# One row of sixteen places for weight units in a trunk layer with a mixture of experts: raw and split units share them, x1's place joins, the second biases run on four row groups, and the experts come in another order

## The chip, the cores and the metric

The kernel runs on one core of a Trainium2 chip. The metric is the device time of one execution in microseconds. Below, PE is the matrix engine, PEld its weight loads, DVE the vector engine, ACT the scalar engine, POOL the GpSimd engine, and SP the queue that issues the weight transfers. SBUF is the memory on the core from which the engines read; PSUM holds the results of products.

## The reference, cut to what matters

The layer takes 512 tokens of 1024 channels. A front part (input projection, a convolution branch, an mLSTM branch, output projection, layer norm) gives x1. Then 4 of 32 experts work on each token, and a second layer norm ends the layer:

```
logits = x1 @ router_w + router_b;  top 4 of 32;  gate = softmax(top 4)
for each expert e, for its tokens:
    h = x1[tok] @ w1[e] + b1[e]              # 1024 -> 2048, halves g and lin
    act = min(g, 7) * sigmoid(1.702 * min(g, 7)) * (clip(lin, -7, 7) + 1)
    acc[tok] += gate * (act @ w2[e] + b2[e])   # 1024 -> 1024
x = layer_norm(alpha * x1 + acc)
```

Everything is float32. An expert has 8 MB of w1 and 4 MB of w2, and all 32 are read: 384 MB.

## The kernel before

**Units.** Weights come in units of 1 MB (128 partitions x 2048 numbers): eight units of w1 (two halves of four: g, then lin) and four of w2 per expert, 384 in all. `Units.fetch` (line 249) issues one transfer on SP's queue into the next of eight raw places: raw2, raw, raw, raw3 three times, hl3 twice. A transfer can start when the last reader of what lay in its place is done, and SP issues in order: one transfer that waits holds all behind it.

**Blocks.** The experts are ranked by how many tokens they have, and a rank has fixed blocks of rows (`RANKS`): rank 0 has two blocks of 128, written (128, 128) below; ranks 1 to 3 have (128, 64); 4 to 7 one of 128; 8 to 12 (64, 32); 13 to 24 one of 64; 25 to 30 one of 32; the first expert in the order has one of 128. In the string `TURNS` these kinds are h (ranks 0 to 3), m, n, l and s. A block of 64 or 32 rows is multiplied in float32 straight from the raw unit (`product`, line 388), two or four column groups of the array side by side. A block of 128 rows needs the unit split into a high and a low half (`split`: ACT casts at line 273, DVE subtracts at line 276), and twelve products of three passes follow (line 400). A split unit takes two places of 8 KB per partition, from six more: hl2 twice and hl four times. A raw unit whose every block is small is held until its products are done; one that is split, until the subtraction is done.

I call an expert with a 128-row block large, and the others small. Each expert's turn on PE is one segment: four units of its w1, two units of the w2 of the expert before it, four units of w1, two units of that w2. A gate (`swiglu`) and turns of rows into columns (`turn`) lie between. `send` adds an expert's result to `ysum` in memory by a scatter on POOL. After the last expert `ysum` is loaded again (line 517) and the layer norm follows.

**Start.** The first eight units are fetched ahead, while the front part ends. The router (`Router.tile`) and the ranking (`Router.order`) run on DVE, ACT and PE. The first expert's first product needs their result.

**Second biases.** `bias2` adds gate-weighted rows of b2 to the sums in `xt`, which holds x1 times alpha (the trace calls this tile hT), and writes `xt` to `ysum`. It brings b2 into rank order by two products (line 1304); then for each of four groups of 128 tokens it turns the 32 gates into a column by one product (line 1310), takes two products with 32 rows of contraction (line 1315) and adds them (line 1317). It stands after the first expert's segment. After it `xt` is free until line 517, and holds 16 KB per partition: two places.

A scheduler of the framework, not the source alone, orders the instructions of each engine.

Of the kernel before, what the change touches and what calls it, by code (L numbers as in the profile page):

```python
# [5 lines left out]
F32 = mybir.dt.float32  # L6
F32R = mybir.dt.float32r
# [8 lines left out]
P = 128; T = 512; D = 1024; NT = 4; KD = 8; E = 32; TOPK = 4; F = 1024  # L16
# [7 lines left out]
def f32(ap):  # L24
    return ap.bitcast(F32)
# [216 lines left out]
class Units:  # L242
# [7 lines left out]
    def fetch(self, src):  # L250
        w = self.raws[self.f % len(self.raws)].tile([P, 2048], F32, name="raw")
        self.f += 1
        self.nc.sync.dma_start(w, src)
        return w
# [22 lines left out]
        return s  # L277

RANKS = [(P, P)] + [(P, 64)] * 3 + [(P,)] * 4 + [(64, 32)] * 5 + [(64,)] * 12 + [(32,)] * 6 + [(P,)]
# [7 lines left out]
    return [(sum(rows[:b]), rows[b]) for b in range(len(rows))]  # L290


TURNS = "lhslmnlhslmlnhslslnmlhslnmlnlsl"


def turns():

    kinds = dict(h=[1, 2, 0, 3], m=list(range(4, 8)), n=list(range(8, 13)), l=list(range(13, 25)), s=list(range(25, 31)))
    return [FIRST] + [kinds[k].pop(0) for k in TURNS]


# [4 lines left out]
def moe(tc, units, ahead, wr, wq, pp, ph, c, R, x1d, ysum, acc, w1, w2, B1, xg, early, bias2, last, xs, ne=E):  # L306
# [3 lines left out]
    nc = tc.nc  # L310
# [160 lines left out]
    for i, r in enumerate(seq):  # L471
        ev = 0 if r == FIRST else nc.sync.value_load(R.perm[0:1, r:r + 1], min_val=0, max_val=ne - 1)
        more = i + 1 < E
        if i == 0:
            gt, oh = gather(seq[1], 0, False)
            x1 = rows(oh)
            gts = [gather(r, 0, False)[0]]
            for t in range(NT):
                nc.scalar.activation(acc[:, t, :], acc[:, t, :], AF.Copy, scale=ALPHA)
        elif more:  # L480
            gt, g = gather(seq[i + 1], 0)
        acts = [width(m) for m in RANKS[r]]
        if acts[0] == F:
            acts = [wq.tile([P, F], F32, name="act", bufs=2)[:, 0:d] for d in acts]
        else:
            act = wq.tile([P, F], F32, name="act", bufs=2)
            acts = [act[:, i * 512:i * 512 + d] for i, d in enumerate(acts)]
        hold = {}
        for h, act, to in zip(gemm1(r, ev, 0, xs, hold), acts, gts):
            swiglu(h, act, 0, to)  # L490
        if pend is not None:
            pe, pa, pg = pend

            hs = [turn(a, *((wr, "xs") if b and a.shape[1] == F else (wq, "hs"))) for b, a in enumerate(pa)]
            ys = places(hs)
            gemm2(pe, 0, hs, ys)
        for h, act, to in zip(gemm1(r, ev, 1, xs, hold), acts, gts):
            swiglu(h, act, 1, to)
        if more:
            gtn, xs = [gt], [turn(g, wr, "xs") if i else x1]  # L500
            for b in range(1, len(blocks(seq[i + 1]))):
                gt, g = gather(seq[i + 1], b)
                gtn.append(gt)
                xs.append(turn(g, wr, "xs"))
        if pend is not None:
            gemm2(pe, 1, hs, ys)
            send(ys, pg)
        if i == 0:
            bias2()
        if i == 1:  # L510
            early()
        pend = (ev, acts, gts)
        if more:
            gts = gtn
# [11 lines left out]
    y = wq.tile([P, F], F32, name="sg", bufs=1)[:, 0:512]  # L526
# [3 lines left out]
    sums = [sums[t // 2][:, t % 2, :] for t in range(NT)]  # L530
# [655 lines left out]
    return B1  # L1186


class Other:


    def __init__(self, pool):
        self.pool = pool

    def tile(self, *_, **__):
        return f32(self.pool.tile([P, 2, 1024], F32R, name="hl")).rearrange("p a b -> p (a b)")


def body(tc, I, out, ne=E):
    nc = tc.nc  # L1200
    top = ExitStack()
# [94 lines left out]

    def bias2():

        b2 = wl.tile([P, D], F32, name="act", bufs=2)[0:E]
        nc.sync.dma_start(b2, I["b2"])  # L1300
        for n in range(2):
            cols = slice(n * 512, (n + 1) * 512)
            ps = pm.tile([P, 512], F32, name="tp", bufs=2)[0:E]
            nc.tensor.matmul(ps, R.sel[0:E, :], b2[:, cols], start=True, stop=True)
            nc.scalar.copy(b2[:, cols], ps)
        for t in range(NT):
            w = wl.tile([P, T], F32, name="gm", bufs=1)
            nc.vector.tensor_add(w[:, 0:E], f32(R.vals[:, t, :, 1]), f32(R.vals[:, t, :, 2]))
            tp = pm.tile([P, 4, P], F32, name="tp", bufs=2)
            nc.tensor.transpose(tp[0:E, 0, :], w[:, 0:E], c["ident"])  # L1310
            wT = w[0:E, P:2 * P]
            nc.scalar.copy(wT, tp[0:E, 0, :])
            for n in range(2):
                ps = pm.tile([P, 512], F32, name="tp", bufs=2)
                nc.tensor.matmul(ps, wT, b2[:, n * 512:(n + 1) * 512], start=True, stop=True)
                x = xt[:, t, n * 512:(n + 1) * 512]
                nc.vector.tensor_add(x, ps, x)
            nc.scalar.dma_start(ysum[t * P:(t + 1) * P], xt[:, t, :])

    fin = {}  # L1320

# [73 lines left out]
```

## Time and profile before

| | before |
|---|---|
| median of 3 runs | 1804.31 us (1802.85 to 1807.08) |
| the profiled execution's own time | 1804.05 us |
| its span, first to last instruction | 1802.2 us |
| mean granted clock of PE | 0.955 of full speed |
| PE, DVE, ACT, POOL busy | 92%, 53%, 31%, 13% |
| moved by DMA | 488.90 MB, mean 271 GB/s |

The busy share of PE is not its distance from a limit: a product that waits for nothing and one in a row of late transfers both count as busy. The line of DMA shares by slice tells more: low for the first 15 slices (the front part), then near 9 with some slices below it. The last weight product ends at 1758 us; what follows is the load of the sums, the layer norm and the stores.

### The profile page before, as it was taken

Reading aid. Unit: us, or ns where it says so; the run is one execution under the profiler, and the core shown is the slowest. Engines: PE = TensorE matmul, PEld = TensorE weight load, DVE = VectorE, ACT = ScalarE, POOL = GpSimd, SP = SyncE. Lnnn points to the kernel's source line nnn. Section 1 sums busy time; section 2 is a strip of 40 time slices with the busy share of each in tenths; the row PEclk is TensorE's granted clock in tenths of the full one; section 3 lists DMA queues with packets and bytes.
Section 4 is the critical chain, followed back from the end, with each engine's and each line's share of the span. In section 5 each row is a group of like instructions: output and inputs, shape, how many; then the busy total and the mean of one; then the engine's idle time right before and its main releaser. Section 6 shows DMA issues by size and latency. Waiting matters only on the chain. (4 is left out here: it accounts for less than half of the span.)

```text
span 1802.2 us, 22812 instructions
## 1 busy us (share of the span) xinstructions
PE 1660.1 (92%) x8840; PEld 1008.7 (56%) x8840; DVE 956.0 (53%) x1431; ACT 557.5 (31%) x739; POOL 237.4 (13%) x174
## 2 busy tenths in 40 slices
PE   7999999899999989989999899997899998999873
PEld 5878878688877836545454443762245543443321
DVE  5999998967567737335253543441135631442104
ACT  4442353334342515223232422320034421321001
POOL 0110031014112001010010200011111111001001
PEclk9999999899999869999999999999899999999986
DMA  5222221122255656999989999589999899999992
GB/s 192 94 71 91 85 94 71 47 94 94 95 182 191 276 192 226 371 402 414 396 303 395 400 415 398 215 334 393 411 414 409 298 357 400 402 360 378 401 400 91
DMA packets 77427, 488.90 MB, mean 271 GB/s; under 512 B 9808, under 2 KB 11616, under 8 KB 22434
## 3 DMA queue, kind: packets, MB, share of 16 engines
q1 hardware_dynamic: 65186, 458.80, 64.0%
q0 software_dynamic: 9104, 19.66, 4.8%
q10 hardware_dynamic: 3024, 8.94, 1.3%
q8 instruction: 71, 1.16, 0.3%
q14 instruction: 42, 0.34, 0.1%
HBM read 471.18 MB, written 19.33 MB: 272 GB/s over the span
## 5 line engine op out<-in xcount | busy, mean ns | idle before, releaser
L276 DVE TENSOR_TENSOR hl<-raw,hl 128x1024 fp32r<-128x1024 f32 x261 | 324.3, 1269 | 133.9 <-ACT hl L273 132.5
L273 ACT CAST hl<-raw 128x1024 fp32r<-128x1024 f32 x261 | 265.0, 1047 | 218.5 <-PE mm L742 78.2
L388 PE MATMUL h<-raw,xs 128*32 128x256 f32 (+1 forms) x2016 | 299.0, 499 | 20.9 <-DMA raw<-w 20.8
L742 PE MATMUL mm<-xhl,hl 128*128 128x512 f32 x1176 | 291.8, 403 | 8.9 <-ACT hl L273 8.9
L400 PE MATMUL h<-hl,xs 128*128 128x512 f32 x1008 | 255.4, 407 | 14.5 <-ACT hl L273 10.2
L742 PEld LDWEIGHTS mm<-xhl,hl 128*128 128x128 f32 x1176 | 224.7, 192 | 64.7 <-ACT hl L273 9.6
L400 PEld LDWEIGHTS h<-hl,xs 128*128 128x128 f32 x1008 | 190.6, 193 | 80.1 <-ACT hl L273 16.3
L388 PEld LDWEIGHTS h<-raw,xs 128*32 128x32 f32 (+1 forms) x2016 | 94.5, 125 | 189.9 <-issue 134.9
L799 DVE SCALAR_TENSOR_TENSOR acc<-zp,vec,acc 128x512 f32<-128x512 f32 x240 | 181.0, 768 | 2.0
L438 DVE TENSOR_SCALAR gm<-h 128x512 f32<-128x512 f32 (+2 forms) x41 | 30.7, 749 | 225.6 <-PE h L388 162.0
L388 PE MATMUL y<-raw,hs 128*32 128x256 f32 (+1 forms) x848 | 128.5, 500 | 9.3 <-DMA raw<-w 8.7
L342 POOL DMA_INDIRECT xg<-x1d,idx x39 | 60.6, 1553 | 550.3 <-DVE oh L325 292.1
L434 DVE TENSOR_SCALAR gm<-h 128x512 f32<-128x512 f32 (+2 forms) x41 | 30.7, 748 | 192.0 <-PE h L388 157.1
L460 POOL DMA_INDIRECT ysum<-yo,idx x40 | 65.8, 1646 | 474.7 <-ACT yo L459 366.1
L400 PE MATMUL y<-hl,hs 128*128 128x512 f32 x432 | 118.2, 419 | 6.7 <-DVE hl L276 3.6
L388 PE MATMUL h<-hl,xs 128*32 128x256 f32 (+1 forms) x672 | 102.3, 498 | 3.8 <-DMA hl<-w 3.8
L400 PEld LDWEIGHTS y<-hl,hs 128*128 128x128 f32 x432 | 80.8, 196 | 39.0 <-issue 10.1
L639 PE MATMUL mm<-hl,xhl 128*128 128x512 f32 x384 | 96.1, 403 | 1.7 <-ACT sg L792 1.5
L388 PEld LDWEIGHTS y<-raw,hs 128*32 128x32 f32 (+1 forms) x848 | 39.1, 124 | 80.6 <-issue 62.4
L639 PEld LDWEIGHTS mm<-hl,xhl 128*128 128x128 f32 x384 | 72.7, 191 | 19.0 <-ACT sg L792 1.8
L459 ACT COPY yo<-y 128x512 f32<-128x512 f32 (+2 forms) x36 | 22.1, 628 | 192.7 <-PE y L388 143.0
L435 ACT ACTIVATE sg<-gm 128x512 f32<-128x512 f32 (+2 forms) x41 | 27.8, 678 | 132.8 <-DVE gm L434 132.6
(309 smaller groups left out, 1594.0 us busy)
## 6 DMA issues: line engine op xcount, KB each, us to landing
raw<-w SPq DMA_DIRECT2D x288, 1024.0 KB
hl<-w SPq DMA_DIRECT2D x96, 1024.0 KB
raw<-wf SPq DMA_DIRECT2D x44, 1024.0 KB
cvp<-xT SPq DMA_DIRECT2D x8, 256.0 KB
hT<-x SPq DMA_DIRECT2D x1, 2048.0 KB
x1d<-hT ACTq DMA_DIRECT2D x4, 512.0 KB
ysum<-hT ACTq DMA_DIRECT2D x4, 512.0 KB
hT<-ysum SPq DMA_DIRECT2D x1, 2048.0 KB
```

Of the source, the lines that this page charges most:

```text
L273: nc.scalar.copy(s[:, 0, :], w)
L276: eng.tensor_sub(s[:, 1, :], w, f32(s[:, 0, :]))
L342: nc.gpsimd.indirect_dma_start(out=g, out_offset=None, in_=split_rows(x1d, m), in_offset=bass.IndirectOffsetOnAxis(ap=ix[:, 0:1], axis=0), ...
L388: nc.tensor.matmul(o[j * m:(j + 1) * m], x[:, 2 * u + k, :], w[:, k * 1024 + j * d:k * 1024 + (j + 1) * d], start=first and k == 0, stop=e ...
L400: nc.tensor.matmul(o[:, j, :], x[:, a, 2 * u + k, :], s[k][:, b, j * 512:(j + 1) * 512], start=first and k == 0 and i == 0, stop=end and k ...
L434: nc.vector.tensor_scalar(gm, h, LIMIT, None, op0=OP.min)
L435: nc.scalar.activation(sg, gm, AF.Sigmoid, scale=SW_ALPHA)
L438: nc.vector.tensor_scalar(gm, h, LIMIT, -LIMIT, op0=OP.min, op1=OP.max)
L460: nc.gpsimd.indirect_dma_start(out=split_rows(ysum, P * d // D), out_offset=bass.IndirectOffsetOnAxis(ap=ix[:, 0:1], axis=0), in_=o, in_of ...
L639: nc.tensor.matmul(ps, src[:, a, kk, t * P:(t + 1) * P], w[k][:, b, :], start=(kk == 0 and (a, b) == PASS[0]), stop=(kk == KD - 1 and (a, ...
L742: nc.tensor.matmul(ps, w[k][:, a, j * P:(j + 1) * P], mov[:, b, k, :], start=(k == 0 and (a, b) == PASS[0]), stop=(k == KD - 1 and (a, b) ...
L799: nc.vector.scalar_tensor_tensor(o, z[:, j:j + T], V("dw_w", m * CT + j), o, op0=OP.mult, op1=OP.add)
```

## The change

`Ring` takes the place of `Units` for the experts: one row of 14 places, from which raw units and split halves take the next in turn (`take`). A raw unit takes one place and a split one two more. When `bias2` is done it adds two places in `xt` at the front of the row (`more`); they take raw units only, since splits pass over them. So there are sixteen.

`bias2` now stands after the first half of the first expert's w1 in the source. The two products that rank b2 write it four times over, on four groups of 32 partitions; the gates of all four groups of tokens are turned by one product; and the products of the four groups of tokens read four row groups of the array and write four banks of PSUM. The write of `xt` to `ysum` follows after all sums.

The order of experts is another one. Before it was, after the first: l h s l m n l h s l m l n h s l s l n m l h s l n m l n l s l, with the (128, 128) expert as the third h. Now it is l m l l s h s n s h l l s h s l n n l l h l l m s n m m n l, with the (128, 128) expert as the first h.

```
+class Ring(Units):
...
+    def take(self, plain=False):
+
+        i = 0
+        while not plain and not isinstance(self.slots[i], tuple):
+            i += 1
+        p = self.slots[i]
+        del self.slots[i]
+        self.slots.append(p)
...
-TURNS = "lhslmnlhslmlnhslslnmlhslnmlnlsl"
+TURNS = "lmllshsnshllshslnnllhllmsnmmlnl"
...
-    kinds = dict(h=[1, 2, 0, 3], m=list(range(4, 8)), n=list(range(8, 13)), l=list(range(13, 25)), s=list(range(25, 31)))
+    kinds = dict(h=[0, 1, 2, 3], m=list(range(4, 8)), n=list(range(8, 13)), l=list(range(13, 25)), s=list(range(25, 31)))
...
+        if i == 0:
+            bias2()
         if pend is not None:
...
-        if i == 0:
-            bias2()
...
-    units = Units(nc, [raw2, raw, raw, raw3, raw3, raw3, Other(hl3), Other(hl3)], [hl2] * 2 + [hl] * 4, set())
+    units = Ring(nc, [(raw2, "raw")] + [(raw, "raw")] * 2 + [(raw3, "raw")] * 3 + [(hl3, "hl")] * 2 + [(hl2, "hl")] * 2
+                 + [(hl, "hl")] * 4)
...
+        b2, p2 = (wl.tile([P, D], F32, name="yo", bufs=2) for _ in range(2))
+        nc.sync.dma_start(b2[0:E], I["b2"])
...
+            nc.tensor.matmul(ps, sel, b2[0:E, cols], start=True, stop=True)
+            nc.scalar.copy(p2[:, cols], ps)
...
+            sums = [y[:, 0, :], y[:, 1, :]] + [pm.tile([P, 512], F32, name="tp", bufs=2) for _ in range(2)]
+            for t in range(NT):
+                part = slice(t * E, (t + 1) * E)
+                nc.tensor.matmul(sums[t], wT[part], p2[part, cols], start=True, stop=True)
+            for t in range(NT):
+                nc.vector.tensor_add(xt[:, t, cols], sums[t], xt[:, t, cols])
         for t in range(NT):
...
             nc.scalar.dma_start(ysum[t * P:(t + 1) * P], xt[:, t, :])
+        units.more([xt[:, 2 * k:2 * k + 2, :] for k in range(2)])
```

Three places show how instructions moved. The first is SP's queue of weight transfers, from the ninth unit on. Before, they stand like this (raw and hl are places, w1 and w2 the weights):

```order
L253 DMA raw_4598<-w1 128x2048
...
L253 DMA raw_4604<-w1 128x2048
...
L253 DMA raw_4610<-w1 128x2048
...
L253 DMA raw_4616<-w1 128x2048
...
L253 DMA raw_4643<-w2 128x2048
...
L253 DMA raw_4663<-w2 128x2048
```

Now, with hT_126 the tile `xt`:

```order
L1322 DMA yo_4437<-b2 32x1024
...
L301 DMA raw_4646<-w2 128x2048
...
L301 DMA hl_4710<-w2 128x2048
...
L301 DMA hT_126<-w1 128x2048
...
L301 DMA hT_126<-w1 128x2048
...
L301 DMA hl_4593<-w1 128x2048
```

Two units of w2 stand ahead; the second expert's first two units of w1 go into `xt`, which `bias2` must have written out by then, and all later units stand behind them.

The second place is PE's queue around `bias2`. Before (selc picks ranks, xs64 is the second expert's input, h_4595 its first result):

```order
L388 MATMUL h_4595<-raw_4616,xs64_4339 64x512 x4
...
L1304 MATMUL tp_4517<-act_4515,selc_3665 32x512
L1304 MATMUL tp_4520<-act_4515,selc_3665 32x512
L1310 MATMUL tp_4525<-ident_69,gm_4523 32x128
L1315 MATMUL tp_4528<-act_4515,gm_4523 128x512
L1315 MATMUL tp_4531<-act_4515,gm_4523 128x512
```

Now (h_4478 is the first expert's second half, h_4580 the second expert's first result):

```order
L431 MATMUL h_4478<-hl_4538,xs_4206 128x512 x6
L1329 MATMUL tp_4442<-yo_4437,gm_4440 128x512
L1329 MATMUL tp_4445<-yo_4437,gm_4440 128x512
L1335 MATMUL tp_4449<-ident_69,gm_4440 128x128
L1344 MATMUL y_4452<-yo_4438,gm_4440 128x512 x2
L1344 MATMUL tp_4453<-yo_4438,gm_4440 128x512
L1344 MATMUL tp_4454<-yo_4438,gm_4440 128x512
...
L419 MATMUL h_4580<-hT_126,xs64_4339 64x512 x8
```

The second expert's first half stood ahead of the biases and now stands behind them, since its weights come into `xt`.

The third place is DVE's queue while the router runs. Before (p0, first and x1T belong to the router):

```order
L155 CAST selb_3669<-sel_3899 128x96
L161 SCALAR_TENSOR_TENSOR p0_3905<-rt_3902,sel_3899 128x1
L162 TENSOR_SCALAR first_3671<-io1_74,p0_3905 128x128
L138 TENSOR_SCALAR x1T_4118<-tp_4120,ln1c_3676 128x128 x4
L143 TENSOR_TENSOR lg_4018<-rt_3991,rb_3659 128x32
```

Now:

```order
L155 CAST selb_3669<-sel_3899 128x96
L307 TENSOR_TENSOR raw_4414<-raw_4274,raw_4414 128x1024
L307 TENSOR_TENSOR raw_4417<-raw_4274,raw_4417 128x1024
L161 SCALAR_TENSOR_TENSOR p0_3905<-rt_3902,sel_3899 128x1
L307 TENSOR_TENSOR raw_4481<-raw_4276,raw_4481 128x1024
L162 TENSOR_SCALAR first_3671<-io1_74,p0_3905 128x128
L307 TENSOR_TENSOR raw_4484<-raw_4276,raw_4484 128x1024
L138 TENSOR_SCALAR x1T_4118<-tp_4120,ln1c_3676 128x128 x4
L143 TENSOR_TENSOR lg_4018<-rt_3991,rb_3659 128x32
L307 TENSOR_TENSOR raw_4499<-raw_4278,raw_4499 128x1024
```

Five subtractions of splits that stood behind the ranking now stand among the router's steps.

## Rows read from the trace of the kernel before

**Rows 1.** The page: busy share of DMA, in tenths, in 40 slices of the span

```profile
DMA  5222221122255656999989999589999899999992
```

**Rows 2.** Stretches: length, busy us (and instructions) by engine, PE clock, DMA share, GB/s

```profile
740.00:1758.00 1018.00, 939.35 (x5738) 464.09 (x5734) 367.95 (x518) 263.70 (x343) 121.00 (x75) 0.97 0.96 377
577.00:740.00 163.00, 151.77 (x706) 95.55 (x706) 96.20 (x183) 59.17 (x78) 10.64 (x16) 0.88 0.69 256
1180.00:1400.00 220.00, 195.66 (x1312) 95.43 (x1305) 62.32 (x105) 50.49 (x70) 27.91 (x19) 0.96 1.02 406
```

**Rows 3.** Stretches of 20 us with low DMA shares

```profile
920.00:940.00 20.00, 20.00 (x93) 12.07 (x93) 12.41 (x14) 8.03 (x9) 3.10 (x2) 1.00 0.62 216
...
1140.00:1160.00 20.00, 20.00 (x115) 13.12 (x114) 9.75 (x9) 7.06 (x9) 0.00 (x0) 1.00 0.31 122
...
1420.00:1440.00 20.00, 20.00 (x91) 12.13 (x88) 12.47 (x16) 8.63 (x10) 1.97 (x1) 1.00 0.68 250
```

**Rows 4.** Waits of SP's queue and of PE: us in total, times, longest

```profile
SPq L253 <- DVE hl L276: 603.2, 100, 31.8
...
PE h L388 <- DMA raw<-w: 20.8, 18, 1.9
PE h L400 <- ACT hl L273: 10.2, 6, 3.3
```

**Rows 5.** PE in order of time: start, length, line, product, records

```profile
693.21 11.32 PE L400 MATMUL h<-hl,xs 128*128 128x512 f32 x48
705.88 3.65 PE L388 MATMUL h<-raw,xs 128*64 128x512 f32 x16
741.30 3.63 PE L388 MATMUL h<-raw,xs 128*32 128x256 f32 x64
```

**Rows 6.** PE from the first expert's products to the end of the biases

```profile
603.06 10.37 PE L400 MATMUL h<-hl,xs 128*128 128x512 f32 x43
...
631.02 2.56 PE L400 MATMUL h<-hl,xs 128*128 128x512 f32 x10
...
637.82 4.50 PE L388 MATMUL h<-raw,xs 128*64 128x512 f32 x18
...
644.72 2.00 PE L1304 MATMUL tp<-act,selc 32*32 32x512 f32 x4 [1.85 <-DMA act<-b]
...
667.66 1.01 PE L330 MATMUL tp<-vals,oh 128*128 128x4 f32 x4
```

**Rows 7.** DVE: the router's steps, a subtraction of a split, an addition of biases

```profile
587.09 0.16 DVE L161 SCALAR_TENSOR_TENSOR p<-rt,sel 128x1 f32<-128x1 f32 x1 [0.39 <-PE rt L159]
590.97 1.37 DVE L138 TENSOR_SCALAR x1T<-tp,ln1c 128x128 f32<-128x128 f32 x4 [2.05 <-PE rt L141]
607.59 1.24 DVE L276 TENSOR_TENSOR hl<-raw,hl 128x1024 fp32r<-128x1024 f32 x1
649.64 0.69 DVE L1317 TENSOR_TENSOR hT<-tp,hT 128x512 f32<-128x512 f32 x1 [6.87 <-PE tp L1315]
```

**Rows 8.** SP's issues of weight units, x their number, around the biases

```profile
639.98 2.71 SPq L253 DMA_DIRECT2D raw<-w  x3
673.68 2.15 SPq L253 DMA_DIRECT2D hl<-w  x2
...
739.04 2.05 SPq L253 DMA_DIRECT2D hl<-w  x2
```

**Rows 9.** The end: last products, scatter, load of the sums, two row groups

```profile
1744.27 1.07 PE L388 MATMUL y<-raw,hs 128*32 128x256 f32 x16 [0.84 <-DMA raw<-w]
...
1746.24 1.58 POOL L460 DMA_INDIRECT ysum<-yo,idx  x1 [27.06 <-ACT yo L459]
...
1756.09 1.94 PE L388 MATMUL y<-hl,hs 128*64 128x512 f32 x8 [0.82 <-DMA hl<-w]
...
1770.35 0.69 PE L537 MATMUL h<-sg,gm 64*128 64x512 f32 x1
1770.36 0.69 PE L537 MATMUL tp<-sg,gm 64*128 64x512 f32 x1
```

More of the change, by code (lines that the diff above doesn't have):

```diff
@@ L277, in split, with __init__, more, fetch @@
         return s
+class Ring(Units):
+    def __init__(self, nc, slots):
+        self.nc, self.slots = nc, deque(slots)
+    def more(self, slots):
+        self.slots.extendleft(slots)
+    def take(self, plain=False):
[5 more added lines that the diff above has]
+        self.slots.append(p)
+        return f32(p[0].tile([P, 2, 1024], F32R, name=p[1])) if isinstance(p, tuple) else p
+    def fetch(self, src):
+        w = self.take(True).rearrange("p a b -> p (a b)")
+        self.nc.sync.dma_start(w, src)
+        return w
+    def split(self, w):
+        s = self.take().bitcast(F32R)
+        self.nc.scalar.copy(s[:, 0, :], w)
+        self.nc.vector.tensor_sub(s[:, 1, :], w, f32(s[:, 0, :]))
+        return s
 RANKS = [(P, P)] + [(P, 64)] * 3 + [(P,)] * 4 + [(64, 32)] * 5 + [(64,)] * 12 + [(32,)] * 6 + [(P,)]
@@ L1186, in bias_rows @@
     return B1
[L1189 to L1196, printed above, removed]
 def body(tc, I, out, ne=E):
@@ L1297, in bias2 @@
     def bias2():
-        b2 = wl.tile([P, D], F32, name="act", bufs=2)[0:E]
-        nc.sync.dma_start(b2, I["b2"])
+        b2, p2 = (wl.tile([P, D], F32, name="yo", bufs=2) for _ in range(2))
+        nc.sync.dma_start(b2[0:E], I["b2"])
+        w = wl.tile([P, F], F32, name="gm", bufs=1)
+        sel = w[0:E, 2 * P:3 * P]
+        nc.vector.tensor_copy(sel.rearrange("p (t e) -> p t e", t=NT), R.sel[0:E, None, :].to_broadcast([E, NT, E]))
         for n in range(2):
             cols = slice(n * 512, (n + 1) * 512)
-            ps = pm.tile([P, 512], F32, name="tp", bufs=2)[0:E]
-            nc.tensor.matmul(ps, R.sel[0:E, :], b2[:, cols], start=True, stop=True)
-            nc.scalar.copy(b2[:, cols], ps)
@@ L1306, in bias2 @@
-        for t in range(NT):
[L1307 to L1317, printed above, removed]
+            ps = pm.tile([P, 512], F32, name="tp", bufs=2)
@@ new lines, in bias2 @@
+            nc.tensor.matmul(ps, sel, b2[0:E, cols], start=True, stop=True)
+            nc.scalar.copy(p2[:, cols], ps)
+        nc.vector.tensor_add(w[:, 0:P].rearrange("p (t e) -> p t e", t=NT), f32(R.vals[:, :, :, 1]),
+                             f32(R.vals[:, :, :, 2]))
+        ps = pm.tile([P, 512], F32, name="tp", bufs=2)
+        nc.tensor.transpose(ps[:, 0:P], w[:, 0:P], c["ident"])
+        wT = w[:, P:2 * P]
+        nc.scalar.copy(wT, ps[:, 0:P])
+        for n in range(2):
+            cols = slice(n * 512, (n + 1) * 512)
+            y = pm.tile([P, 2, 512], F32, name="y", bufs=1)
+            sums = [y[:, 0, :], y[:, 1, :]] + [pm.tile([P, 512], F32, name="tp", bufs=2) for _ in range(2)]
[4 more added lines that the diff above has]
+                nc.vector.tensor_add(xt[:, t, cols], sums[t], xt[:, t, cols])
```

## The prediction, made before the changed kernel ran

> **What bounds the kernel now.** I read the DMA shares by slice first [rows 1], then the same by stretches, then the waits, then PE in order of time. From 740 us to the last weight product at 1758 the transfers run at a mean share of 0.96 and 377 GB/s, where a stretch in which they never stop shows 1.02 and 406 [rows 2]. So over 1018 us they stood still for about (1.02 - 0.96) / 1.02 x 1018 = 60 us. The stops lie together: three of the nine worst stretches of 20 us are in [rows 3], and the worst run, 1120 to 1180, is the segment of the (128, 128) expert. There PE is busy all the time and DMA at 0.31. SP waits mostly for subtractions that free a raw place [rows 4]. In the stretches between, PE waits for weights. So the limit changes hands: under a large expert PE is the bound and all eight raw places are full; under small ones the transfers are, and eight units of lead are soon used up. A larger lead is worth what the 60 us of stops are worth.
>
> Prices. A unit on a 128-row block takes PE 11.32 / 4 = 2.83 us, on 64 rows 3.65 / 2 = 1.82, on 32 rows 3.63 / 4 = 0.91 [rows 5] (a float32 product leaves two records: 16 are two units of a 64-row block, 64 are four of a 32-row block). A unit costs the transfers: 377 GB/s x 1018 us = 384 MB for the 347 units after 740, gathers and scatters among it, is 1.106 MB each, and at 406 GB/s 2.72 us. A segment of 12 units is 32.7 us of transfers. On PE, with some 3 us of turns, gathers and biases, a segment is 57 to 64 us for (128, 128), 47 to 51 for (128, 64), 34 to 38 for m and n, 21 to 28 for l, 17 to 20 for s behind a small one.
>
> **Term 1: the start.** Five subtractions of 1.24 us now stand among the router's steps. The first of them stands where p is at 587.09; DVE was idle 2.05 us for PE before x1T [rows 7], which swallows part of three or four. I take +3 us for the first expert's first product, so 606 for 603.06 (bounds 1 and 6). One of its splits now stands behind the gate of its first half on DVE: I take 4 us of wait on PE (0 to 6). Its products end at 633.6 before [rows 6], so near 641 now. Then the chain of the biases: 2.0 us for the ranking products [rows 6], two copies and a turn, some 1.7, four products side by side 1.0, eight additions of 0.69 [rows 7] with a second round of products among them, 6.5, and a subtraction of a w2 split that stands ahead of the additions, 1.5: sums complete near 653.5. Writing 2 MB at 406 GB/s is 5.2 us, with landing 6.5: the place is free near 660. Only then can SP issue the second expert's first unit, which lands after 2.72 + 2: PE goes on near 665. Before, it went on at 667.66 [rows 6], but had the second expert's first four units (8.5 us with the gather among them, up to 642.3) behind it. So PE stands 5 to 6 us later in its work.
>
> That the four products run side by side rests on the end of the trace: two products on two row groups into two banks start 0.01 us apart, and each takes 0.69 us [rows 9]. The Trainium skill (TensorEngine Tiling (Array Packing), "Gotcha 1: PSUM Pressure") says that row tiles can't use the same PSUM bank at once; here each group has a bank of its own, so by that rule too they run together. By it, if a bank were shared, the two rounds would cost eight products of 1.0 us for two, and the start 6 us more; the trace shows the first case for two groups, and nothing here shows four.
>
> For the transfers: before, 22 units were issued by 642.7, nothing till 673.7, and 38 by 734.4, which had landed by 740, with two more at 739 [rows 8]. Now 10 are issued by 645, nothing till 660, then one every 2.72 us, since no early segment stops them for long (l, m, l, l follow): 10 + (740 - 662) / 2.72 = 38.7 at 740. Equal: 0 us (bounds -8 and +15, three units and five).
>
> **Term 2: stops in the steady part.** From a given unit the row of places reaches sixteen units ahead if they are small, and 16 / 3 = five if they are large. At the end of a large expert come four small units, two of its w2 (three places each) and four small ones: 14 places, ten units. So while PE is in a (128, 128) segment of 57 us the lead can grow from three units to ten, and the transfers bring 12 + 7 = 19 units, 52 us: a stop of 5 for the 28.6 us of 1120 to 1180 before ([rows 3] for its middle). In a (128, 64) segment of 47 to 51 us they bring 17 or 18 units, 46 to 49 us: 0 to 3 us each, three times. The segments of m and n are 1 to 5 us above 32.7: what the lead doesn't take there, some 8 us over eight. One blocked transfer holds all behind it on SP, and a place that waits for a product of five units ago frees late at the entry of a large expert, where the old kernel had eight raw units and three split ones: some 10 us over nine large experts. Together 5 + 5 + 8 + 10 = 28, say 30 us for 60: -30 us (bounds -50 and 0).
>
> Splits reach five units ahead on PE where six places reached three, and so PE's waits for casts [rows 4] may fall by some us. No row shows such a row of places; I take 0.
>
> **Term 3: the end.** Before, the transfers were the bound to the last unit: PE waits 0.84 us before the s expert's last unit, whose product ends at 1745.3, 0.82 before the last of all [rows 9]; from 1745.3 to the end, through scatter and load, it is 56.9 us. That chain stays. Now m m n l n l stand at the end: PE takes 37.5 + 37.9 us for 65.4 of transfers in the two m segments, and 62 in the last two. So it ends with a lead of some three units: the last expert but one is done 3 x 2.72 = 8 us later against the last transfer than before. It sends two blocks for one, and a scatter holds POOL 1.58 us [rows 9]. +10 us (bounds 0 and +14).
>
> **Sum.** 1802.2 + 0 - 30 + 10 = 1782.2 us of span; the execution's time is 1.85 above its span, 1784; the median of the runs is 0.3 above that execution. I say **1785 us**.
>
> From PE's side: 120 units x 2.83 + 240 x 1.82 + 132 x 0.91 = 897 us, 3% more on the large ones for mixing (10), some 110 of turns, gathers and biases, less the first expert's 26: 991 from 665. To this come 37 us of waits for ACT and DVE like those of before (the largest of twelve is in [rows 4]) and 22 for the first five segments, whose 58 transfers still to come take 158 us against 136 on PE: 665 + 991 + 37 + 22 = 1715, and the chain to the end, 56.9 + 1.6 less the 7.3 us of the last expert's w2, gives 1766. PE and transfers are thus within 16 us of each other, and whoever is not the bound in one segment cannot hand all of it on: neither sum is reached from below.
>
> **The rivals.** *The transfers hardly stop.* If SP's order costs nothing and the lead covers m and n, the stops are 10 us and the end +4: 1802.2 - 50 + 4, or 1758 with what lies around. For it: the sum from PE's side. Against: the 5 us under the (128, 128) expert are bound by the places.
>
> *PE takes the place of the transfers.* If its waits for casts and subtractions double because a split now waits for a place that a product frees, PE's sum is 1766 + 37 = 1803: no change. For it: DVE frees most raw places [rows 4], and both now come from one row. Against: the five units ahead.
>
> *Slower: five units are too few at the entry of a large expert.* There the row of places gives up what the old kernel had ready, eight raw units and three split. Each of the nine large experts after the first would then stop the transfers while PE splits. With stops of s us each, the sum is -60 + 9 s + 10: from s = 5.6 on the kernel is slower, and with 8 us, the stop of the old kernel's (128, 64) segments (47 to 51 us for 12 units and three of lead), it is 1826. Against: at the places where it would strike the transfers are the bound anyway and the lead is near zero in both.
>
> That the row is not sixteen places long because the scheduler holds `xt` back is excluded by SP's order: units go into hT_126 throughout.
>
> **How the numbers follow.** Forecast (1772 to 1799): 0.50. Transfers hardly stop (1745 to 1772): 0.23. PE takes over (within 0.2% of 1804): 0.13. Slower: 0.14. The range goes from 1750, which leaves out some 0.06 of the second case, to 1816, which leaves out some 0.09 of the last. A measurement of this kernel can tell 0.2%, 3.6 us, from no change; so faster 0.73, same 0.13, slower 0.14.
>
> **What would show it.** Right: PE's first product near 606 and the end of the biases' wait near 665; DMA share 0.99 or more from 670 on, with dips only under the (128, 128) expert (now near 850) and at entries of large experts; last weight product near 1730 with a lead at the end. Term 1 is wrong if the first transfer into hT is issued after 670 or fewer than 36 units have landed by 740; term 2 if the share from 740 to the last product stays at 0.96 or rises to 1.02; term 3 if PE still waits for the last units. The forecast as a whole is wrong if PE's waits for casts, 10.2 us for the largest [rows 4], grow past 40.

## The result, and the profile after

The changed kernel takes **1821.2 us** (median of 4 runs, 1814.17 to 1826.68) against 1803.58 us for the kernel before on the same chip: a ratio of 1.0106 (95% interval 1.0085 to 1.0126). It is slower, where 1785 us was forecast. The profiled execution's span is 1821.7 us against 1802.2, 19.5 more. In `kernel.py` of after most lines stand 31 further down: L388 is L419, L400 is L431, L253 is L301.

In the line of DMA shares the four slices from 546 us on, the start, are at 4, 1, 5 and 8, where [rows 1] has 5, 6, 5 and 6. Later the deepest are a 6 and a 7 under (128, 64) experts, where [rows 1] has a 5 under the (128, 128) expert:

```profile
DMA  5212212132364158999999889699997899989982
```

The stretches that answer to [rows 2] and [rows 3] (columns as there; 1773.33 is the end of the last weight product):

```profile
577.00:740.00 163.00, 133.44 (x621) 93.54 (x623) 91.76 (x176) 55.02 (x71) 12.47 (x17) 0.82 0.60 227
740.00:1773.33 1033.33, 943.23 (x5805) 484.04 (x5818) 371.42 (x522) 262.27 (x346) 132.53 (x75) 0.97 0.95 375
1140.00:1160.00 20.00, 14.56 (x57) 7.56 (x55) 3.94 (x7) 2.58 (x3) 5.13 (x3) 0.83 0.37 125
1380.00:1400.00 20.00, 19.67 (x82) 13.49 (x83) 11.09 (x17) 5.65 (x7) 4.64 (x3) 0.86 0.35 103
860.00:880.00 20.00, 20.00 (x114) 15.17 (x114) 12.64 (x16) 6.18 (x7) 1.52 (x1) 1.00 0.86 326
```

From these lines the time can be split without a rest: span = 740 + (bytes after 740) / 406 GB/s + what stands still beside that + last product to end. Before: 377 x 1018 = 383.8 MB, 945 us, stops 73, end 44.2. After: 375 x 1033.3 = 387.5 MB, 954 us, stops 79, end 48.4. So the start costs 9 us, the stops 6, the end 4. The rates are rounded to 1 GB/s, so the first two are good to some 2 us; by the bytes moved from 577 to 740 us (41.7 and 37.0 MB) the start costs 11.6. (The stops of before are 73 us by rates, 377 of 406 GB/s; the prediction's 60 is by shares, 0.96 of 1.02.) The two rows of 20 us from 1140 and 1380 lie in (128, 64) experts; the one from 860 is the (128, 128) expert.

The stretches around the (128, 64) experts behind 740 us, two in before and three in after:

```profile
900.00:960.00 60.00, 59.57 (x351) 31.51 (x348) 32.50 (x39) 22.56 (x29) 9.20 (x5) 1.00 0.84 318
1400.00:1460.00 60.00, 58.41 (x314) 32.67 (x311) 36.02 (x40) 21.81 (x25) 7.17 (x4) 1.00 0.79 287
```
```profile
970.00:1070.00 100.00, 90.90 (x472) 49.09 (x473) 43.52 (x56) 30.96 (x39) 16.66 (x6) 0.97 0.83 332
1120.00:1200.00 80.00, 70.67 (x407) 41.57 (x401) 38.71 (x56) 26.33 (x34) 17.72 (x6) 0.90 0.80 321
1380.00:1460.00 80.00, 79.67 (x358) 42.89 (x359) 37.08 (x46) 24.12 (x30) 8.48 (x5) 0.97 0.77 300
```

Against 406 GB/s these are stops of 13 and 18 us in before, and of 18, 17 and 21 in after. The third (128, 64) expert of before lay ahead of 740 us.

The start, all engines (SPq and ACTq are issues):

```profile
587.71 1.99 ACT L306 CAST raw<-raw 128x1024 fp32r<-128x1024 f32 x2 [2.81 <-DMA raw<-w]
588.79 3.07 DVE L307 TENSOR_TENSOR raw<-raw 128x1024 fp32r<-128x1024 f32 x2 [1.27 <-ACT raw L306]
591.99 3.62 PE L141 MATMUL rt<-rw,x1T 128*128 128x32 f32 x16 [4.25 <-DVE p L161]
...
611.25 1.20 PE L431 MATMUL h<-hl,xs 128*128 128x512 f32 x4
...
623.86 0.33 SPq L301 DMA_DIRECT2D raw<-w  x1
...
645.71 0.34 SPq L301 DMA_DIRECT2D hl<-w  x1
...
658.58 2.90 ACTq L1348 DMA_DIRECT2D ysum<-hT  x4
...
665.31 0.96 SPq L301 DMA_DIRECT2D hT<-w  x2
...
673.43 2.83 PE L419 MATMUL h<-hT,xs 128*64 128x512 f32 x6 [3.54 <-DMA hT<-w]
```

The subtractions among the router's steps (L307) waited for casts that waited for weights, and the router's own step p and PE behind it waited with them. The first product is at 611.25 (603.06 in [rows 6]). SP issues one unit at 623.86, one at 645.71, and then stands until the second biases are written: the load into x1's place (hT) goes out at 665.31, and PE goes on at 673.43 (667.66 in [rows 6], with half an expert more behind it).

The steady part, at the last (128, 64) expert. L406 turns the first block's rows, L397 the second's, L361 finds which rows a block takes, POOL L373 is a gather, L431 is a 128-row block's product, L419 a small one's:

```profile
1363.93 33.73 SPq L301 DMA_DIRECT2D raw<-w  x4
...
1372.46 1.09 PE L406 MATMUL tp<-ident,xg 128*128 128x128 f32 x8
...
1379.69 2.07 PE L431 MATMUL h<-raw,xs 128*128 128x512 f32 x4 [2.20 <-ACT xs L407]
1381.69 1.02 PE L361 MATMUL tp<-vals,oh 128*128 128x4 f32 x4
...
1384.35 1.97 POOL L373 DMA_INDIRECT xg<-x1d,idx  x1 [22.04 <-DVE oh L356]
...
1394.08 0.60 PE L397 MATMUL tp<-ident,xg 128*128 128x128 f32 x4
...
1395.36 1.94 PE L419 MATMUL h<-raw,xs 128*64 128x512 f32 x8 [0.33 <-ACT xs L398]
...
1397.12 1.89 PE L419 MATMUL h<-hT,xs 128*64 128x512 f32 x8
...
1399.05 0.33 SPq L301 DMA_DIRECT2D hT<-w  x1
```

The first block is turned 7 us ahead of its first product. The second block's gather needs the result of L361, which stands on PE behind the first block's first products; so it goes out at 1384.35, and the block's first product comes at 1395.36. Until then the expert's raw units are held. SP's four issues from 1363.93 end at 1397.66; its next goes into hT, right after the product at 1397.12 that read the hT unit.

Waits that answer to [rows 4] (us in total, times, longest):

```profile
SPq L301 <- PE h L419: 205.7, 60, 22.2
...
PE h L431 <- ACT xs L407: 13.9, 5, 4.3
...
PE tp L397 <- DMA xg<-x1d,idx: 12.9, 3, 6.9
```

At L301, SP now waits most for PE's products on small blocks. The last two lines have no match among the larger waits of before: PE waits for its input's casts and for second gathers. The end, as against [rows 9]:

```profile
1766.24 7.09 PE L419 MATMUL y<-hl,hs 128*64 128x512 f32 x32 [0.98 <-ACT yo L490]
...
1784.82 5.36 PE L563 MATMUL h<-hT,ident 128*128 128x512 f32 x8 [8.82 <-DMA hT<-ysum]
```

PE waits for no weights here.

### The profile page after: what moved, and what is told of

Same layout as the page of the kernel before. It is cut to its first block, busy times and chain, and to the rows that moved or that the text cites. A ratio compares the mean times of both kernels' runs of the same rounds, so it can differ in the third digit from the quotient of the medians.

```text
span 1821.7 us, 22765 instructions
## 1 busy us (share of the span) xinstructions
PE 1643.3 (90%) x8820; PEld 1024.7 (56%) x8837; DVE 954.3 (52%) x1429; ACT 552.0 (30%) x736; POOL 253.6 (14%) x174
## 5 line engine op out<-in xcount | busy, mean ns | idle before, releaser
L419 PE MATMUL h<-hl,xs 128*32 128x256 f32 (+1 forms) x1312 | 193.2, 489 | 8.8 <-DMA hl<-w 8.5
L431 PE MATMUL h<-hl,xs 128*128 128x512 f32 x576 | 154.4, 417 | 13.3 <-ACT xs L407 6.1
L373 POOL DMA_INDIRECT xg<-x1d,idx x39 | 72.0, 1846 | 617.0 <-DVE oh L356 238.7
L276 DVE TENSOR_TENSOR hl<-raw,hl 128x1024 fp32r<-128x1024 f32 x89 | 118.4, 1335 | 58.4 <-ACT hl L273 58.3
L419 PE MATMUL h<-raw,xs 128*32 128x256 f32 (+1 forms) x920 | 134.7, 501 | 14.1 <-DMA raw<-w 13.0
L431 PEld LDWEIGHTS h<-hl,xs 128*128 128x128 f32 x576 | 110.8, 198 | 46.3 <-ACT xs L407 6.6
L419 PEld LDWEIGHTS h<-hl,xs 128*32 128x32 f32 (+1 forms) x1312 | 64.1, 123 | 118.2 <-issue 91.1
L273 ACT CAST hl<-raw 128x1024 fp32r<-128x1024 f32 x89 | 92.6, 1047 | 110.9 <-PE mm L773 75.6
L431 PE MATMUL h<-raw,xs 128*128 128x512 f32 x432 | 116.7, 420 | 7.8 <-ACT xs L407 7.8
L431 PEld LDWEIGHTS h<-raw,xs 128*128 128x128 f32 x432 | 85.0, 201 | 31.6 <-ACT xs L407 8.6
L307 DVE TENSOR_TENSOR hl<-hl 128x1024 fp32r<-128x1024 f32 x70 | 83.0, 1218 | 29.8 <-ACT hl L306 29.6
L419 PE MATMUL y<-hl,hs 128*32 128x256 f32 (+1 forms) x624 | 93.0, 490 | 3.3 <-DMA hl<-w 1.2
L419 PEld LDWEIGHTS h<-raw,xs 128*32 128x32 f32 (+1 forms) x920 | 44.5, 126 | 87.8 <-issue 55.2
## 6 DMA issues: line engine op xcount, KB each, us to landing
raw<-w SPq DMA_DIRECT2D x131, 1024.0 KB, 18.2
hT<-w SPq DMA_DIRECT2D x70, 1024.0 KB, 15.8
```

The lines of the kernel that those rows point to most:

```text
L273: nc.scalar.copy(s[:, 0, :], w)
L276: eng.tensor_sub(s[:, 1, :], w, f32(s[:, 0, :]))
L307: self.nc.vector.tensor_sub(s[:, 1, :], w, f32(s[:, 0, :]))
L373: nc.gpsimd.indirect_dma_start(out=g, out_offset=None, in_=split_rows(x1d, m), in_offset=bass.IndirectOffsetOnAxis(ap=ix[:, 0:1], axis=0), ...
L419: nc.tensor.matmul(o[j * m:(j + 1) * m], x[:, 2 * u + k, :], w[:, k * 1024 + j * d:k * 1024 + (j + 1) * d], start=first and k == 0, stop=e ...
L431: nc.tensor.matmul(o[:, j, :], x[:, a, 2 * u + k, :], s[k][:, b, j * 512:(j + 1) * 512], start=first and k == 0 and i == 0, stop=end and k ...
```

## The experiments

All ratios are to the kernel before, timed beside each run. MB are what was moved from 577 to 740 us; "stops" and "end" as above, from the profiled execution.

| run | us | ratio (95%) | MB to 740 | stops | end |
|---|---|---|---|---|---|
| before | 1803.6 | | 41.7 | 73 | 44 |
| after | 1821.2 | 1.0106 (1.0085 to 1.0126) | 37.0 | 79 | 48 |
| e1 new order alone | 1788.5 | 0.9924 (0.9899 to 0.9948) | 45.2 | 61 | 50 |
| e2 one row of 14 alone | 1825.8 | 1.0138 (1.0116 to 1.0160) | 36.5 | 84 | 44 |
| e3 second biases alone | 1795.1 | 0.9960 (0.9945 to 0.9974) | 44.5 | 67 | 43 |
| e4 after, no x1's place | 1788.8 | 0.9927 (0.9907 to 0.9947) | 44.5 | 64 | 47 |
| e5 after, x1's places at the back | 1802.1 | 0.9998 (0.9983 to 1.0013) | 41.9 | 64 | 49 |
| e6 order and biases, two rows of before | 1772.1 | 0.9821 (0.9805 to 0.9837) | 49.4 | 58 | 49 |
| e7 two rows, x1 in front | 1799.4 | 0.9980 (0.9969 to 0.9991) | 42.2 | 67 | 48 |
| e8 two rows, x1 at the back | 1775.4 | 0.9832 (0.9808 to 0.9855) | 51.2 | 71 | 47 |
| e9 after, two passes | 1766.8 | 0.9800 (0.9762 to 0.9838) | 39.1 | 29 | 52 |
| e10 two rows, 5 raw and 9 split | 1832.0 | 1.0174 (1.0138 to 1.0211) | 42.5 | 97 | 52 |
| e11 after, second gather tile | 1808.1 | 1.0039 (1.0021 to 1.0057) | 37.3 | 60 | 48 |
| e12 e6, second gather tile | 1773.2 | 0.9857 (0.9824 to 0.9890) | 49.1 | 56 | 50 |
| e13 row of 14 from the second expert on | 1800.9 | 0.9994 (0.9981 to 1.0008) | 45.3 | 72 | 49 |
| e14 the same with x1's places | 1784.1 | 0.9899 (0.9873 to 0.9925) | 47.4 | 64 | 48 |
| e15 e6, two passes | 1721.3 | 0.9557 (0.9532 to 0.9582) | 53.6 | 9 | 50 |
| e16 after, rows gathered earlier | 1785.0 | 0.9904 (0.9889 to 0.9919) | 36.5 | 39 | 48 |
| e17 e8, rows gathered earlier | 1764.9 | 0.9792 (0.9771 to 0.9812) | 51.5 | 55 | 49 |
| e18 e6, rows gathered earlier | 1780.2 | 0.9877 (0.9858 to 0.9896) | 48.2 | 58 | 49 |

**Which part is it?** e1, e2 and e3 make one part of the change alone in the kernel before, as in the diff ahead; e4 takes one part away:

```
-        units.more([xt[:, 2 * k:2 * k + 2, :] for k in range(2)])
```

> The kernel before with nothing but the new order of experts. Theory A (the loss is in the start and in the single row of places, where a raw place that is held blocks the freed places behind it; the order by itself is worth little): 1796 to 1810 us, within 0.4% of before, with dips in the DMA share of 10 to 15 us at each of the four large experts. Theory B (the order is the loss, since it sets the two-block and the 128-row experts closer together): 1815 us or more, and the dips stand at the same experts as in the changed kernel.

> The kernel before with its two rows of places (eight raw, six split) made one row of the same 14, old order and old second biases, x1's place not added. Theory A: the row is worse than two rows at the (128,64) experts, where the second block's rows come late and raw units stay held; four large experts at 10 to 20 us each, less what a free choice of places gives at the small ones: 1815 to 1840 us. Theory C (what is short is the number of places, and one row uses them at least as well as two): 1790 to 1804 us.

> The kernel before with the second biases' new products at their new place alone; two rows of places, old order, x1's place not added. Theory A: the rewrite is cheap by itself, since SP's queue does not wait for it when no unit goes into x1's place: 1798 to 1806 us, the share of the DMA engines between 577 and 740 us near the 0.69 of before. Theory D (the rewrite at this place is what costs the start): 1812 to 1820 us, and that share near the 0.60 of the changed kernel.

> The changed kernel without x1's place: 14 places in the one row. Theory A: the start gets back up to 10 us since no load waits for the second biases, and the steady part loses the reach of two units, some 2 x 2.6 us at each of about nine experts with two blocks: 1830 to 1850 us. Theory D (the start is the whole loss, and places beyond 14 bring little): 1805 to 1812 us.

The order gains 0.8%, so theory B falls, but A's range missed too. The second biases gain 0.4%, so D falls; A's range is missed by 3 us. The row of 14 loses 24 us in the old order, as A said. For e4 both theories were wrong: without x1's place the kernel is 32 us faster, not slower. Two more places cost more than any other part of the change.

**x1's places, and one row against two.** e5 puts x1's places at the back of the row; e6 puts the two rows of before back (no x1's place); e7 and e8 have those two rows with x1's places joined to the raw one, in front or at the back:

```
e5, e8:
-        self.slots.extendleft(slots)
+        self.slots.extend(slots)
e6 (7 and 8 with x1's places):
-    units = Ring(nc, [(raw2, "raw")] + ...
+    units = Units(nc, [raw2, raw, raw, raw3, raw3, raw3, Other(hl3), Other(hl3)], [hl2] * 2 + [hl] * 4, set())
```

> The changed kernel with x1's two places added at the back of the row, so that fourteen other places are taken before a load has to wait for the second biases' write. Theory A (x1's places cost by standing at the head of SP's queue in the start): the start is that of the row of 14, the steady part has two places more: 1776 to 1790 us, DMA share 577 to 740 us near 0.73. Theory E (16 places, two of which splits pass over, run worse in the steady part than 14): 1800 to 1812 us, with the start repaired but the dips at the (128,64) experts as deep as in the changed kernel (0.37 and 0.35 in the worst slice).

> The changed kernel with the two rows of before (eight raw, six split) in place of the one row, x1's place not used: new order and new second biases together. If the two parts add (order 13 us, second biases 7): 1779 to 1785 us. If the row of 14 is worth nothing either way in the new order: the 1788.8 us of the row of 14, within 3 us. If both parts win the same time: 1788 to 1795 us.

> The changed kernel with two rows, raw and split apart as before; x1's two places go to the front of the raw row (ten raw places). Theory A: the start keeps the loss of the changed kernel, some 18 us (first load into x1's place waits for the second biases), and the steady part has a raw lead of ten units even at large experts: 1790 to 1800 us, share from 740 us on at 0.98 or more. Theory C (the lead is what counts, and it is the same in sum): 1815 us or more.

> The same two rows with x1's two places at the back of the raw row, so that eight loads go ahead of the first that waits for the second biases. Theory A: start as in the row of 14 and a steady lead of ten raw units: 1765 to 1780 us, the fastest of all. If lead brings nothing more once the order is new: 1779 to 1787 us, like the two rows without x1's place.

The stretch from 577 to 740 us in e4, e6, e7 and e8, in this order:

```profile
577.00:740.00 163.00, 143.51 (x698) 97.64 (x700) 101.09 (x189) 61.40 (x80) 14.33 (x18) 0.88 0.73 273
```
```profile
577.00:740.00 163.00, 149.84 (x743) 98.48 (x742) 101.13 (x190) 65.60 (x83) 13.92 (x18) 0.92 0.80 303
```
```profile
577.00:740.00 163.00, 139.40 (x668) 94.43 (x669) 94.02 (x180) 57.07 (x74) 15.10 (x17) 0.85 0.67 259
```
```profile
577.00:740.00 163.00, 151.27 (x726) 99.86 (x726) 101.31 (x189) 63.67 (x79) 12.95 (x17) 0.90 0.81 314
```

By 645 us SP had issued 22 units in before and e6, 16 in e4, 13 in e5 and 9 in after and e7: in one row the first expert's splits take places that loads had, and in front x1's places hold the queue.

Order and second biases together gain 31 us, more than the 20 of their sum; 19 of them (49.4 - 41.7 MB at 406 GB/s) lie in the start. With x1's places in front this gain is gone: 227 GB/s with one row, 259 with two. In front against at the back costs 19 us with one row (after, e5) and 24 with two (e7, e8); of the former 12 are the 4.9 MB that move later, of the latter 22 are 9 MB. So the wait for the second biases' write costs some 12 us of start with one row and 22 with two, against what the rest of the change gives there. And with the same sixteen places two rows (e8) are 27 us faster than one (e5), of which 23 are the start (41.9 against 51.2 MB). But ten raw places (e8) are no faster than eight (e6): the start is better by 1.8 MB and the stops are longer by 13 us. Of the forecasts, e5 has the time of theory E but not the repaired start of either (41.9 MB for 44.5 in e4), e6 is faster than all three, e7 has A's time but a share of 0.96 from 740 us on, not 0.98, and e8 has A's time without being the fastest.

**Whose time are the stops?** e9 and e15 leave one of three passes out for split units; e10 moves three places from the raw row to the split one; e11 and e12 gather second blocks into a tile of their own:

```
e9, e15:
-                for i, (a, b) in enumerate(PASS):
+                for i, (a, b) in enumerate(PASS[:2]):
e10:
+    units = Units(nc, [raw2, raw, raw, Other(hl3), Other(hl3)], [hl2] * 2 + [hl] * 4 + [Named(raw3)] * 3, set())
e11, e12:
-        g = xg[:, 0:width(m)]
+        g = (xg2 if b else xg)[:, 0:width(m)]
```

> The changed kernel with two of the three passes of products on split units (the third, low half of the input with high half of the weights, is left out, so the result is rougher): PE has a third less to do at the large experts, 120 units x 2.83 / 3 = 113 us; transfers, casts, places and the order stay. Theory A (the stops of the transfers are PE's time showing through places that are held: PE's own work is the bound of the steady part): 1730 to 1775 us, share from 740 us on 0.99 or more. Theory C (the row's turns and the transfers bind, PE's products beside them): 1795 us or more.

> Two rows of 14 places in all, as in the run with eight raw and six split places (1772.1 us), but five raw and nine split: the lead at a large expert is then that of one row of 14 (14 / 3, some five units), and at a small one five instead of 14. If the short lead at large experts is what makes the one row slow (1788.8 us with 14 places): as slow or slower, 1788 to 1810 us. If it is the strict turn of raw and split places in one row (a place that is held stops those behind it): faster than the one row, 1772 to 1784 us.

> The changed kernel with a second tile for the gathered rows of second blocks, so that this gather need not wait for the first block's turn. Theory A2 (the deep dips at the (128,64) experts come from the second block's rows arriving late, while raw units are held for them): 1795 to 1808 us, and PE's waits for gathered rows (12.9 us at the turn of 64 rows) near 0. If the late rows are only a follow-up of PE standing still for other reasons: 1817 to 1824 us.

> New order and new second biases with the two rows of before (1772.1 us), and the second tile for gathered rows. In that kernel PE waits only 2.4 us for gathered rows: 1768 to 1774 us; if the gathers of second blocks also free other work earlier: 1762 to 1768 us.

> New order, new second biases and two rows (1772.1 us), with two of three passes on split units (the third is left out, so the result is rougher): PE has 113 us less. In that kernel the transfers stand still some 49 us between 740 us and the last product (share 0.97 of 1.02). If these stops are PE's time under large experts, they go, and the rest is the transfers': 1725 to 1740 us. If the transfers were the bound and the stops the places': 1760 us or more.

From 740 us on, first e9, then e15:

```profile
740.00:1718.50 978.50, 874.31 (x5372) 398.84 (x5384) 368.54 (x518) 260.08 (x343) 122.44 (x73) 0.95 0.99 394
```
```profile
740.00:1661.03 921.03, 836.58 (x5230) 376.08 (x5240) 355.70 (x500) 251.91 (x330) 110.54 (x71) 0.97 1.01 402
```

With an estimated 113 us less for PE the stops fall by 50 us in both and the time by 54 and 51: stops under large experts are PE's time. But after stays 46 us slower than two rows (49 with all passes), so what one row with x1's places in front loses against two rows is not PE's products. e10: with five raw places the kernel is 60 us slower than with eight, and slower than both forecasts, so five raw places in two rows are too few. Whether a held place that stops those behind it costs something in one row, it doesn't show. e11 gets 13 us back and takes stops from 79 to 60 with the start unchanged, and PE's wait at the second turn goes from 12.9 us to 2.4. At the last (128, 64) expert nothing changes: there L361 stands behind the first products as before, at 1361.69, and the gather goes out at 1363.84. In two rows there is nothing to get (e12).

**How much is the start?** e13 and e14 use two rows for the first expert's twelve units and one row from then on; e14 adds x1's places at its back:

```
+        if self.slots is None and self.n == 24:
+            self.slots = deque(list(self.rows[1]) + list(self.rows[0]) + self.extra)
```

> The changed kernel without x1's place (1788.8 us), but the first expert uses the two rows of before; the one row of 14 begins after its last split. The traces put 12 of the one row's 17 us to the start (273 against 303 GB/s between 577 and 740 us, 4.9 MB at 406 GB/s) and 5 to 7 to the rest. If that reading is right: 1774 to 1780 us. If the row loses at the large experts: 1785 to 1790 us.

> The same with x1's two places joined to the row at its back after the first expert, when the second biases are long written out: sixteen places and nothing waits for them in the start. If x1's places cost only by their wait in the start: as the run with 14 places, within 4 us, or faster. If they cost in the steady part (two rows: 3 us slower with them, one row: 13): 1785 to 1795 us.

e13 is a miss: it is slower than e4, not faster. The start isn't repaired (45.3 MB): SP has issued 21 units by 645 us, for 22 in e6, but 27 by 700 us for 34, so the loss moves to where the row begins. And the stops are longer by 8 us. So my split of the one row's cost was wrong. e14 is 17 us faster than e13: x1's places are worth something in one row when nothing waits for them.

**Why PE is late at large experts.** In e6, at the same expert as above, the turn stands 30 us ahead (L406), the second gather and turn come long before the products, and small and large products alternate, so raw units become free one by one:

```profile
1306.09 1.09 PE L406 MATMUL tp<-ident,xg 128*128 128x128 f32 x8
...
1310.67 1.05 POOL L373 DMA_INDIRECT xg<-x1d,idx  x1 [20.41 <-DVE oh L356]
...
1325.13 0.66 PE L397 MATMUL tp<-ident,xg 128*128 128x128 f32 x4
...
1335.97 0.73 PE L431 MATMUL h<-hl,xs 128*128 128x512 f32 x2 [0.27 <-ACT hl L273]
...
1338.83 1.94 PE L419 MATMUL h<-raw,xs 128*64 128x512 f32 x8
```

Of the seven large experts after 740 us, the first block's turn stands 15 to 29 us ahead of the first product in before, 14 to 35 in e6, 4 to 16 in e8, and in after 35 at the (128, 128) expert, 18 at the last and 2 to 7 at the other five. This order is fixed when the program is built. e16, e17 and e18 gather rows one expert earlier, with two tiles in turn:

```
-            gt, g = gather(seq[i + 1], 0)
+            gt, g = soon or gather(seq[i + 1], 0)
+            soon = gather(seq[i + 2], 0) if i + 2 < E - 1 else None
```

In these three, the expert behind one with two blocks works on the rows of the expert that follows it, since the tile is written again before its turn; the instructions and their sizes are the same.

> The changed kernel (1821.2 us) with the next expert's rows gathered one expert earlier, into the one of two tiles that is free, so that turns stand further ahead of large experts. If late turns and late second gathers make the deep stops: 1798 to 1806 us, at least as good as a second tile for second blocks alone (1808.1), with PE's waits for its input's casts (13.9 us) under 5. If the short reach of the row alone makes them: 1815 to 1825 us.

> Two rows with x1's places at the back (1775.4 us), rows gathered one expert earlier. There the turn stands 1 to 15 us ahead of large products and PE idles 77 us after 740 us, 17 more than without x1's places. If late turns take what ten raw places should give: 1758 to 1768 us, the fastest. If not: 1773 to 1778 us.

> Two rows of 14 places (1772.1 us), rows gathered one expert earlier; here turns are 10 to 32 us ahead already. Theory of late turns: no gain, 1769 to 1775 us. If earlier rows help by themselves: 1760 to 1768 us.

e16, its two stretches, those of the three (128, 64) experts, then the expert of above (lines stand one further down):

```profile
577.00:740.00 163.00, 132.93 (x623) 92.01 (x626) 91.75 (x179) 54.70 (x71) 14.26 (x18) 0.83 0.61 224
740.00:1734.98 994.98, 938.59 (x5800) 475.08 (x5810) 370.57 (x519) 262.51 (x346) 120.00 (x74) 0.97 0.98 390
960.00:1060.00 100.00, 98.76 (x613) 49.39 (x606) 46.06 (x63) 32.75 (x43) 10.96 (x8) 1.00 1.00 403
1100.00:1180.00 80.00, 74.44 (x509) 39.96 (x503) 37.40 (x51) 27.56 (x34) 9.36 (x6) 0.98 1.01 406
1340.00:1420.00 80.00, 77.71 (x355) 40.78 (x354) 43.35 (x54) 30.52 (x37) 13.72 (x5) 0.98 0.84 329
...
1325.65 0.60 PE L407 MATMUL tp<-ident,xg 128*128 128x128 f32 x4
...
1337.30 0.66 PE L407 MATMUL tp<-ident,xg 128*128 128x128 f32 x4
...
1341.81 1.66 PE L432 MATMUL h<-raw,xs 128*128 128x512 f32 x6
```

The start is as bad as in after, and yet the kernel is 36 us faster: the stops fall from 79 to 39 us, and PE's wait for its input's casts from 13.9 to 3.7 us. The turn now begins 14 and 27 us ahead at the first two (128, 64) experts, for 2 and 4 in after, and their stops of 18 and 17 us are gone (403 and 406 GB/s). At the last it begins 16 us ahead, but its second half stands 4.5 us ahead, and 15 of 21 us of stop remain (329 GB/s). So late turns and late second gathers made about half of the stops of after. Of these 40 us e11 alone, whose tile for second blocks e16 has too, takes 19. Late turns are not all: in e2 they stand 13 to 37 us ahead at six of the seven large experts and the stops are 84 us, and in e14 3 to 6 us at five of them and the stops are 64. e17 gains 10 us from the same edit. e18, where turns were early, loses 8; I expected no change, and didn't find out why (3 of them lie in the start, by 1.2 MB). The fastest kernel with all three passes that computes the reference is e6 at 1772.1 us, 1.8% faster than before.

## Why the prediction was wrong, step by step

**What bounds the kernel.** That the limit changes hands, and that stops under large experts are PE's time, held (e9, e15).

**Term 1 (start), forecast 0, measured +9 to +12 us.** The chain to the release of x1's place was right, its sizes were short: first product 611.25 for 606, because a subtraction among the router's steps waits for its cast and that for its weights, where I counted only its own 1.24 us; load into hT at 665.31 for 660; PE on at 673.43 for 665. By 740 us 32 units had landed (the 33rd at 741.0) for the forecast 38.7 and the limit of 36 that I had set. Two of these 6.7 units are the 5 us of late release. For the others the step that failed is "one every 2.72 us, since no early segment stops them for long": between 666 and 740 us SP stood for 11.9 us behind a product of the first expert's w2, and for 11.9 behind a table that DVE makes and whose transfer goes through the same queue (0.5 in before):

```profile
SPq L301 <- PE y L431: 13.0, 3, 11.9
SPq L1113 <- DVE act L1112: 11.9, 1, 11.9
```

The larger failure is what I compared with. In the start of before the transfers stood still too, and the new order and second biases alone would have filled 19 us of that (e6). I gave those two parts no gain of their own, and so took the wait at x1's place for free. Four products on four row groups do run together, as assumed:

```profile
652.22 1.22 PE L1344 MATMUL y<-yo,gm 32*128 32x512 f32 x2 [3.02 <-ACT gm L1337]
652.23 1.22 PE L1344 MATMUL tp<-yo,gm 32*128 32x512 f32 x2
```

Each product leaves two records; the first ones of all four start within 0.02 us, and the round of four is over at 654.3, after 2.1 us. In before two such products, one behind the other, took 3.8 (L1315). The forecast 1.0 us a round was the length of one record. The second round ends at 658.95, with the first round's additions ahead of it.

**Term 2 (stops), forecast -30 us, measured +4 to +6.** The (128, 128) expert is as forecast: some 6 us of stop for the forecast 5 and the 28.6 of before. The three (128, 64) experts were put at 0 to 3 us each; they stop for 17 to 21, no less than in before. The step that failed is the sentence on 47 to 51 us per segment, with raw units becoming free along the way. PE takes its input later there: turns stand right ahead of the products, second gathers behind them, and the expert's units are held meanwhile. With early turns sixteen places do bring stops of 39 us (e16) for the 73 of before, but 12 of these 34 come with the new order alone (e1); against two rows of 14 with early turns (e18) they bring 19. The order of the changed kernel's PE queue was there to be read before the run; I read it around the second biases and not at the large experts. The rival "five units are too few at the entry of a large expert" came nearest (1826 us at 8 us each), and e10 shows that five raw places are too few in two rows. But 56 of the 79 us sit in three experts of nine, and early turns take about half of the 79 away without one more place.

The rival in which PE's waits for casts double did not come: the largest wait for a cast, 13.9 us, is for the input's, where I had set 40 as the limit; the largest for a split unit's is 3.8.

**Term 3 (end), forecast +10, measured +4** from the last product on. My split counts PE's lag behind the last transfer among the stops; with it the end is +8: from the last unit's landing, 1767.4 us, it is 54.3 us for 46.1 in before (where PE waited for that unit until 1756.09). PE had all its weights at the end, as forecast. The order of experts ends with n m m l n l, and not as the forecast and the list of kinds ahead of it have it.

**The sum.** 9 + 6 + 4 = 19 us for the forecast -20. The order of experts, which had no term, is a gain of 13 us alone in the old kernel; the second biases, of 7.

What stays open: why turns stand later with more places (e6 and e8; e4 and e5) in the order that is fixed when the program is built; why one row has longer stops than two even with early turns (e2); why e13 is slower than e4; and why ten raw places with late turns lose 13 us of stops against eight.

## What to carry to other kernels

When buffers are added, read the new order on the engine that uses them, at the places where it is the bound, and not only the order of the loads: here the input's turn moved from 15 to 29 us ahead of the products to 2 to 7 at five of seven large experts, and late turns and second gathers cost 40 us of stops, more than sixteen places gave. A buffer that becomes free only after a write should not stand at the head of an in-order queue; put it at the back, so that other loads go first. And price a wait against the time that the rest of the change gives at that place, not against the old kernel alone.

## What the runs showed that I had not expected

Where transfers run through, they move about the same in several variants: 406 GB/s over 220 us in before, 402 over 921 us in e15, 403 and 406 over 100 and 80 us in e16. A unit's median time from issue to landing in after is 15.8 to 18.2 us by place; at 2.72 us a unit that makes an estimated six loads in flight. And the parts of a change didn't add: order and second biases gain 13 and 7 us alone and 31 together; the one row costs 24 us in the old order and 17 in the new one.
